# A hybrid decoder step: sample states in four row groups, small products grouped, first slice reloaded

## The chip, the cores and the metric

One core of a Trainium2 chip runs the whole step. The metric is the device time of one execution in microseconds, as the median of several runs.

## The reference

One layer on 256 prompt tokens and 8 samples of 8 tokens, 320 columns in all, of width 2048. Nine conditioning vectors go through a weight of 2048 x 12288 and give scales, shifts and gates for every feature. The layer then does the following:

```python
h = rmsnorm(x, g_pre_mix) * (1 + sc1) + sh1
q, k, v, g, u, vs = split(h @ w_in)            # six parts of 1024
o, S = retention(rotary(q), rotary(k), v, s0)  # 8 heads of 128; S = S*gamma^n + k^T v
vn = layernorm(gelu(vs), ln_g, ln_b)
m = concat([silu(g) * layernorm(o), gelu(u) * spatial_gate(vn)]) @ w_o
x = x + gt1 * rmsnorm(m, g_post_mix)
h2 = rmsnorm(x, g_pre_ffn) * (1 + sc2) + sh2
x = x + gt2 * rmsnorm(square(relu(h2 @ w_ff1)) @ w_ff2, g_post_ffn)
```

The outputs are x for prompt and samples, the retention states S of the prompt and of each of the 8 samples, and vn of the samples. A sample's new state is its old one times gamma to the 8, plus the sum over its 8 tokens of k (with a decay) times v.

## The kernel before, in words

Everything is kept with features on the 128 partitions and the 320 tokens as columns. A large product (`mm3`, line 320) is in three parts: weight and activation are each split into a high and a low half of the type fp32r, and high by high, high by low and low by high are added up in a bank of PSUM. A weight piece of up to 128 x 2048 is loaded into one of two raw buffers; `half_w` (line 294) has ScalarE cast 1024 columns of it (`wh`) and VectorE subtract that from the raw ones (`wl`), in one of three pairs of buffers. Main tiles take four banks of PSUM in turn (`new_acc`), the adaptive weights have one, and all small products share three (`small`).

The input projection runs over slices of its 16 row blocks, of 1, 2, 5 and 8 blocks (`CHUNKS`), and in each slice over 40 column tiles (`N_ORDER`); partial sums are kept in `z` and added up by VectorE. In the last slice a tile is done when its sum is, and `after_tile` (line 631) starts what depends on it: the spatial gate, and after tiles 13, 19, 25 and 31 the retention of a pair of heads (`ret_pair`, line 501). In between, `steps` loads pieces of the adaptive weights, and when four are there `flush` (line 255) issues their products, 16 calls in four column groups of the array, then VectorE's transposition of the result (`ada_drain`), four small products that sum it (`ada_sums`, tile `adaT`) and the scaling (`ada_scale`).

`ret_pair` does for each of two heads: rotation of q and k, transposes of v (`pv`) and k (`pk`), scores (`sc`), outputs (`po`), statistics. At its end come the sample states: for each two of the eight samples GpSimd masks the transposed v by sample (`ve`), TensorE multiplies it with the transposed k, 64 rows for each head (`pn`), and VectorE adds the result to the old state (line 580). After every second pair `ret_norm` (line 596) normalises and transposes the outputs, one head after the other.

`first_slice` (line 673) is the first of the four slices: five pieces of eight tiles, each in a raw buffer of its own of which it fills half, loaded and cast when the tile before has been issued.

A planner (the tile framework) orders each engine's instructions: it simulates times and takes ready work by its place in the program. `tc.high_priority` lets work go earlier (`ahead()` by 500 places), `tc.keep_in_program_order` fixes an instruction behind those fixed before it, and `tc.issue_after(i)` puts instructions behind i on its engine. Each engine's queue, and SyncE's queue of transfers, is then worked off in that order. Most calls go through helpers, so the profile shows line 112 for `tt`, 324 to 326 for `mm3` and 300 for the cast. A matmul in fp32 is two instructions in the trace, and a transpose in fp32 one.

Of the kernel before, what the change touches and what calls it, by code (L numbers as in the profile page):

```python
# [8 lines left out]
F32 = mybir.dt.float32  # L9
# [72 lines left out]
def hybrid_step(ctx: ExitStack, tc, A, O):  # L82
# [66 lines left out]
    bm = cst[:, 208:240].rearrange("p (q b) -> p q b", q=4)  # L149
# [72 lines left out]
    def ada_finish(feats, acc):  # L222
        ada_scale(*ada_sums(*ada_drain(feats, acc)))

    def ada_sums(feats, part):

        nf = len(feats)
        ncol = P * nf
        pv = part[:, :ncol].rearrange("p (i q r) -> p i q r", i=nf, q=4)
        pt = small("adaT")  # L230
        for q in range(4):
            PE.matmul(pt[32 * q : 32 * q + 32, : 9 * nf], sel, pv[:, :, q, 0:9], start=True, stop=True, tile_position=(0, 32 * q))  # L232
        return feats, pt

    def ada_scale(feats, pt):
# [12 lines left out]
    class Ada:  # L248


        def __init__(self, groups):
            self.left = list(groups)
            self.ws = []

        def flush(self, pin=False):
            if self.ws and len(self.ws) == len(self.left[0]):
                feats = self.left.pop(0)
                acc = ps_ada.tile([P, 512], F32, tag="ada", name=nm("ada"))
                with tc.high_priority():
                    ada_products(feats, self.ws, acc, pin)  # L260
                ada_finish(feats, acc)
                self.ws = []

        def products(self, acc):

            feats = self.left.pop(0)
            assert len(self.ws) == 4
            ada_products(feats, self.ws, acc)
            self.ws = []
            return feats, acc  # L270

# [229 lines left out]
    def ret_pair(qkv, pr, o, mv):  # L501

        kts, vts = slot("kts"), slot("vts")
        os_ = slot("os")
        s0s, s0qs = [], []
        for e in range(2):
            h = 2 * pr + e
            q, k, v = qkv[e]
# [10 lines left out]
            pv = small("pv")  # L519
            for t in range(2):  # L520
                PE.transpose(pv[:, P * t : P * (t + 1)], v[:, P * t : P * (t + 1)], ident)
            PE.transpose(pv[:nr, 256:384], v[:, c0:T], ident)
            vt = slot("vt")
            V.tensor_copy(vt[:, :256], pv[:, :256])
            V.tensor_copy(vts[rw, :128], pv[rw, 256:384])
# [3 lines left out]
            PE.transpose(pk[:nr, 256:384], k[:, c0:T], ident)  # L529
            kt = slot("kt")  # L530
            for t in range(2):
                S.activation(kt[:, P * t : P * (t + 1)], pk[:, P * t : P * (t + 1)], AF.Copy, scale=sdec[:, 2 * h + t : 2 * h + t + 1])
# [33 lines left out]
            s0s.append(s0)  # L566
            s0qs.append(s0q)
        for i in range(4):
            ve = slot("ve")
            tt(ve[:, :256].rearrange("p (b e) -> p b e", b=2), vts[:, :128].unsqueeze(1).broadcast_to([P, 2, P]),  # L570
               bm[:, pr, 2 * i : 2 * i + 2].unsqueeze(2).broadcast_to([P, 2, P]), ALU.mult, G)
            pns = [small("pn") for _ in range(2)]
            for e in range(2):
                rw = slice(64 * e, 64 * e + 64)
                PE.matmul(pns[e][:, :256], kts[rw, :128], ve[rw, :256], start=True, stop=True)  # L575
            for e in range(2):
                h = 2 * pr + e
                g8 = float((1.0 - 2.0 ** (-5.0 - h)) ** NS)
                sb = s0s[e][i][:, :256]
                V.scalar_tensor_tensor(out=sb, in0=sb, scalar=g8, in1=pns[e][:, :256], op0=ALU.mult, op1=ALU.add)  # L580
                if i == 3:
                    nc.sync.dma_start(O["ss"][h], s0qs[e][:, :, :256])
        return os_

    later = []
# [10 lines left out]
    def ret_norm(hs, o, oss, mv):  # L596
        rs = tp.tile([P, 12], F32, tag="rs12", name=nm("rs12"))
        rsqrt_(rs, mv[:].rearrange("p h t c -> p (h t) c")[:, :, 1], 12)
        for h in hs:
            os_ = oss[(h % 4) // 2]  # L600
            pt = small("oT")
            for t in range(3):
                src = o[h][:, P * t : P * (t + 1)] if t < 2 else os_[:, P * (h % 2) : P * (h % 2) + P]
                i = 3 * (h % 4) + t
                V.tensor_scalar(src, src, mv[:, h % 4, t, 0:1], rs[:, i : i + 1], op0=ALU.subtract, op1=ALU.mult)
                PE.transpose(pt[:, P * t : P * (t + 1)], src, ident)
            ot = slot("oT")
            S.copy(ot[:, :TP], pt[:, :TP])
            V.tensor_copy(ijs(ot[:, TP:]), rows_ijs(pt[:, 256:384]))
            oT[h] = ot  # L610


    z = {}
# [59 lines left out]
    def first_slice():  # L673

        nt = _per_piece(0)
        mod1(0, V, True)
        ws = [w_in_piece(0, last_ins[0].ins), w_in_piece(1)]
        steps(ada_a, 3)
        for ti, f in enumerate(N_ORDER):
            if ti % nt == 0 and nt <= ti < ZT - nt:  # L680
                ws.append(w_in_piece(ti // nt + 1))
            if ti == nt:
                steps(ada_a, 1)
            if ti == 21:
                ada_a.flush(True)
                steps(ada_a, 2)
            if ti in (28, 31):
                mod1(len(hx), V, True)
            if ti == 30:
                ws.append(w_in_piece(ZT // nt))  # L690
            if ti == 35:
                ada_a.flush(True)
                steps(ada_a, 2)
            acc = new_acc()
            mm3(acc, ws[ti // nt][ti % nt], hx[0], True, True)
            z[f] = slot("z")
            if ti % 3 == 2:
                V.tensor_copy(z[f], acc[:, :T])
            else:
                S.copy(z[f], acc[:, :T])  # L700
        return ws[-1]

    w0 = first_slice()
    piece = -(-ZT // _per_piece(0))
# [224 lines left out]
    for c in range(NC_FF):  # L929
        act = [None] * KB  # L930

        def done_1(m, acc):
            rl, a = slot("rl"), slot("a")
            if c == 0 and m < 8:
                u = us[m] if m < 4 else evict_1(acc)
                tt(u[:, :T], u[:, :T], r2, ALU.mult)
                tt(sam(u), sam(u), u[:, T + 1 : T + 9].unsqueeze(2).broadcast_to([P, NB, NS]), ALU.add)
                S.activation(rl[:, :TP], u[:, :TP], AF.Relu, bias=u[:, T : T + 1])
                S.activation(rl[:, TP:], u[:, TP:T], AF.Relu)
            else:  # L940
                S.activation(rl, acc[:, :T], AF.Relu)  # L941
            tt(a, rl, rl, ALU.mult, G)
            act[m] = split(a)

        if c == 0:
            steps(ada_c, 4)
            for i in range(4):
                done_1(i, acc_1[i])
            h2 = []

            def extra(n):
                steps(ada_c, 1)
                for f in range(len(h2), min(len(h2) + n, KB)):
                    h2.append(modulate(x1[f], r2, A2, SH2, f))

            project("w_ff1", 0, 8, hs, nat, (4,), lambda: extra(2), done_1, 4)
            project("w_ff1", 0, KB, h2, nat, (8,), lambda: extra(4), done_1, 8)
        else:
            project("w_ff1", 16 * c, KB, h2, nat, (), lambda: None, done_1)

        def done_2(m, acc):
            if c == 0:
                if m == 0:
                    steps(ada_c, 100)
                if m % 4 == 0:
# [11 lines left out]
    assert not ada_c.left  # L977
# [9 lines left out]
def _consts():  # L987
# [24 lines left out]
            cst[:, 128 + 2 * h + t] = gam[h] ** (TP - 1 - (P * t + np.arange(P))) * sc  # L1012
        cst[:, 144 + 8 * h : 152 + 8 * h] = gam[h] ** (np.arange(NS) + 1.0)
    for pr in range(4):
        for b in range(NB):
            for e in range(2):
                col = np.where(sb == b, gam[2 * pr + e] ** (NS - 1.0 - ss), 0.0) * sc
                cst[64 * e : 64 * e + 64, 208 + 8 * pr + b] = col

    tri = np.zeros((P, 192))  # L1020
    tri[:, :P] = np.arange(P)[None, :] >= np.arange(P)[:, None]
# [87 lines left out]
```

## Time and profile before

| | |
|---|---|
| median of 3 runs | 1573.48 us (1573.41 to 1573.91) |
| profiled execution | 1572.06 us |
| its span, first to last instruction | 1570.1 us |
| mean granted TensorE clock | 0.995 |
| TensorE busy | 1540.7 us |
| VectorE busy | 817.9 us |
| ScalarE busy | 591.3 us |
| GpSimd busy | 174.3 us |

Busy time counts an engine as busy while one of its instructions is recorded; matmuls are recorded with their fill and drain, so that neighbours overlap. The time between the starts of two neighbours shows what one costs.

### The profile page before, as it was taken

To read this page: it belongs to the slowest core of one execution; us is meant where nothing else is said; L and a number is where in the kernel's file an instruction comes from. 1 tells how busy PE (TensorE), PEld (TensorE's weight loads), DVE (VectorE), ACT (ScalarE), POOL (GpSimd) and SP (SyncE) were. 2 spreads that over 40 slices of the span, in tenths; PEclk is the share of its full clock that TensorE was granted. 3 is DMA by queue.
4 is the path that set the end of the run, shared out by engine and by line. 5 is a ranking of instruction groups with operands and counts; after the bars stand their busy time and mean duration, and the time that the engine had idled before them with its cause. 6 is when DMAs were issued, how large, how long until landed. Compare 5 with 4: busy or idle time off the path is not lost.

```text
span 1570.1 us, 25814 instructions
## 1 busy us (share of the span) xinstructions
PE 1540.7 (98%) x10852; PEld 1441.7 (92%) x10852; DVE 817.9 (52%) x1367; ACT 591.3 (38%) x891; POOL 174.3 (11%) x198
## 2 busy tenths in 40 slices
PE   8999999999999999999999999999999999999995
PEld 6798898888899998789999999999999999999995
DVE  5776566677744446676433344444444444444555
ACT  5332236233433334454433344322344223443331
POOL 0000000001000111044100121000112000121210
PEclk9999999999999999999999999999999999999998
DMA  8988886765777635884434344443434444343442
GB/s 354 379 309 325 312 333 237 251 245 184 275 287 276 265 134 202 322 314 168 147 149 160 137 161 143 153 154 142 161 138 158 148 148 158 138 161 139 157 149 80
DMA packets 57156, 323.92 MB, mean 206 GB/s; under 512 B 5584, under 2 KB 18128, under 8 KB 22096
## 3 DMA queue, kind: packets, MB, share of 16 engines
q1 hardware_dynamic: 56464, 320.98, 54.9%
q8 instruction: 85, 1.39, 0.3%
q10 hardware_dynamic: 576, 1.29, 0.2%
q14 instruction: 31, 0.25, 0.0%
HBM read 314.65 MB, written 7.60 MB: 205 GB/s over the span
## 4 chain that ended last, share of the span: by engine, by line
PE 90%; issue 4%; DVE 2%; POOL 1%; DMA 1%; ACT 1%; SPq 0%; DVEq 0%; POOLq 0%; ACTq 0%
PE acc L324 27%; PE acc L326 27%; PE acc L325 27%; PE ada L204 5%; POOL mt L112 1%; DVE f L112 1%; PE pn L575 1%; DMA adaw<-in_w_ada_dram 1%; DMA x<-in_x_dram 1%; DVE wl L112 0%; POOL a L112 0%; DVE z L112 0%; PE gate L469 0%; PE po L553 0%; PE adaT L232 0%
## 5 line engine op out<-in xcount | busy, mean ns | idle before, releaser
L324 PE MATMUL acc<-hi,wh 128*128 128x320 f32 x2944 | 913.1, 310 | 2.6 <-ACT wh L300 1.5
L326 PE MATMUL acc<-hi,wl 128*128 128x320 f32 x2944 | 910.6, 310 | 1.1 <-DVE wl L112 1.0
L325 PE MATMUL acc<-lo,wh 128*128 128x320 f32 x2944 | 910.7, 310 | 0.0
L112 DVE TENSOR_TENSOR wl<-raw,wh 128x1024 fp32r<-128x1024 f32 (+1 forms) x386 | 470.7, 1220 | 477.3 <-ACT wh L300 462.6
L300 ACT CAST wh<-raw 128x1024 fp32r<-128x1024 f32 (+1 forms) x386 | 402.9, 1045 | 731.7 <-PE acc L325 679.9
L324 PEld LDWEIGHTS acc<-hi,wh 128*128 128x128 f32 x2944 | 553.1, 188 | 13.5 <-issue 7.0
L326 PEld LDWEIGHTS acc<-hi,wl 128*128 128x128 f32 x2944 | 553.0, 188 | 8.9 <-issue 6.7
L325 PEld LDWEIGHTS acc<-lo,wh 128*128 128x128 f32 x2944 | 553.0, 188 | 4.3 <-issue 3.9
L112 POOL TENSOR_TENSOR a<-rl 128x320 f32<-128x320 f32 x64 | 84.2, 1315 | 683.3 <-ACT rl L941 631.1
L204 PE MATMUL ada<-adaw,csil 128*32 128x512 f32 (+1 forms) x800 | 88.0, 578 | 1.2 <-DMA adaw<-in_w_ada_dram 1.2
L112 DVE TENSOR_TENSOR z<-z,acc 128x320 f32<-128x320 f32 x120 | 57.3, 485 | 55.9 <-PE acc L326 55.3
L112 POOL TENSOR_TENSOR sq<-sq,sq 128x320 f32<-128x320 f32 x28 | 39.5, 1411 | 279.7 <-ACT sq L779 279.6
L112 DVE TENSOR_TENSOR lo<-a,hi 128x320 fp32r<-128x320 f32 x64 | 32.1, 502 | 67.9 <-ACT hi L333 67.9
L204 PEld LDWEIGHTS ada<-adaw,csil 128*32 128x32 f32 x800 | 23.6, 109 | 47.3 <-issue 43.6
L333 ACT CAST hi<-a 128x320 fp32r<-128x320 f32 x64 | 29.4, 459 | 90.1 <-POOL a L112 90.1
L112 DVE TENSOR_TENSOR f<-f,acc 128x320 f32<-128x320 f32 x48 | 23.4, 488 | 68.2 <-PE acc L326 68.2
L325 PE MATMUL acc<-lx,wh 128*128 128x330 f32 x128 | 40.5, 317 | 0.6 <-DVE lx L112 0.6
L326 PE MATMUL acc<-hx,wl 128*128 128x330 f32 x128 | 40.6, 318 | 0.0
L324 PE MATMUL acc<-hx,wh 128*128 128x330 f32 x128 | 39.1, 320 | 0.0
L112 POOL TENSOR_TENSOR ve<-vts,cst 128x256 f32<-128x256 f32 x16 | 14.0, 898 | 175.7 <-PE sc L537 74.7
L112 POOL TENSOR_TENSOR mt<-mt,A 128x64 f32<-128x64 f32 x23 | 11.2, 485 | 177.5 <-DVE A L246 176.0
L326 PEld LDWEIGHTS acc<-hx,wl 128*128 128x128 f32 x128 | 24.2, 189 | 2.6 <-issue 2.5
(183 smaller groups left out, 716.6 us busy)
## 6 DMA issues: line engine op xcount, KB each, us to landing
raw<-in_w_ff_dram SPq DMA_DIRECT2D x128, 1024.0 KB, 4.8
adaw<-in_w_ada_dram SPq DMA_DIRECT2D x96, 1024.0 KB, 7.8
raw<-in_w_in_dram SPq DMA_DIRECT2D x33, 1024.0 KB, 5.7
raw<-in_w_o_dram SPq DMA_DIRECT2D x16, 1024.0 KB, 4.8
raw<-in_w_in_dram SPq DMA_DIRECT2D x13, 960.0 KB, 6.0
s<-in_s_dram SPq DMA_DIRECT2D x8, 512.0 KB, 5.8
out_ss_dram<-s SPq DMA_DIRECT2D x8, 512.0 KB, 4.0
x<-in_x_dram SPq DMA_DIRECT2D x4, 640.0 KB, 6.7
```

Source lines behind the costliest of these rows:

```text
L112: return (eng or V).tensor_tensor(out=out, in0=a, in1=b, op=op)
L204: mm = PE.matmul(acc[32 * j : 32 * j + 32, :ncol], csil[:, kb, :], ws[kb // nk][:, kb % nk * ncol : (kb % nk + 1) * ncol], start=i < 4, st ...
L300: ins = S.copy(wh[:, :n], r)
L324: PE.matmul(acc[:, :n], wh, ah, start=start, stop=False)
L325: PE.matmul(acc[:, :n], wh, al, start=False, stop=False)
L326: PE.matmul(acc[:, :n], wl, ah, start=False, stop=stop)
L333: S.copy(hi, src)
L575: PE.matmul(pns[e][:, :256], kts[rw, :128], ve[rw, :256], start=True, stop=True)
```

## The change

Four things are changed.

In `ret_pair`, the sample states are multiplied in four row groups of 32 rows, each of which holds the four samples of one half of one head. ScalarE makes four masks of 128 columns for each pair (`bm` has four columns for each pair now), each of which serves all row groups. Products go to three small banks and, as the fourth, one bank of the main tiles, 512 columns each; VectorE updates the states in four instructions of 512 columns, at a higher priority. The transposes of k are put before those of v, which are kept in program order.

In `Ada`, a lazy instance (`ada_b` and `ada_c`) issues the small sums of one batch right behind the products of the next one, kept in program order.

In `ret_norm`, six transposes of two heads are issued together, the last one first.

In `first_slice`, pieces are loaded two to a raw buffer, four ahead; the adaptive loads are put between them; casts are issued at given tiles, behind the latest copies of results on their engines.

```diff
@@ Ada
+        def sums(self, pin=False):
+            if self.drained:
+                ada_scale(*ada_sums(*self.drained, pin))
+            self.drained = None
...
                 with tc.high_priority():
                     ada_products(feats, self.ws, acc, pin)
-                ada_finish(feats, acc)
+                if self.lazy:
+                    with tc.high_priority():
+                        self.sums(True)
+                    self.drained = ada_drain(feats, acc)
+                else:
+                    ada_finish(feats, acc)
...
-    ada_a, ada_b, ada_c = Ada(g_pre), Ada(g_gt1 + g_ffn), Ada(g_gt2)
+    ada_a, ada_b, ada_c = Ada(g_pre), Ada(g_gt1 + g_ffn, True), Ada(g_gt2, True)
@@ ret_pair
-        for i in range(4):
-            ve = slot("ve")
-            tt(ve[:, :256].rearrange("p (b e) -> p b e", b=2), vts[:, :128].unsqueeze(1).broadcast_to([P, 2, P]),
-               bm[:, pr, 2 * i : 2 * i + 2].unsqueeze(2).broadcast_to([P, 2, P]), ALU.mult, G)
-            pns = [small("pn") for _ in range(2)]
-            for e in range(2):
-                rw = slice(64 * e, 64 * e + 64)
-                PE.matmul(pns[e][:, :256], kts[rw, :128], ve[rw, :256], start=True, stop=True)
...
+        ve = [slot("ve")[:, :256].rearrange("p (b e) -> p b e", b=2) for _ in range(2)]
+        for j in range(4):
+            S.activation(ve[j // 2][:, j % 2, :], vts[:, :128], AF.Copy, scale=bm[:, pr, j : j + 1])
+        pns = [small("pn") for _ in range(3)] + [new_acc()]
+        for c in range(2):
+            for g in range(4):
+                rg = slice(32 * g, 32 * g + 32)
+                PE.matmul(pns[g][:, 256 * c : 256 * c + 256], kts[rg, :128], ve[c][rg].rearrange("p b e -> p (b e)"),
+                               start=True, stop=True, tile_position=(32 * g, 0))
+        for e in (1, 0):
+            h = 2 * pr + e
+            g8 = float((1.0 - 2.0 ** (-5.0 - h)) ** NS)
+            with ahead():
+                for i in (1, 0):
+                    sb = s0qs[e][:, 2 * i : 2 * i + 2, :256]
+                    V.scalar_tensor_tensor(out=sb, in0=sb, scalar=g8, in1=pns[2 * e + i].rearrange("p (b e) -> p b e", b=2), op0=ALU.mult, op1=ALU.add)
+            nc.sync.dma_start(O["ss"][h], s0qs[e][:, :, :256])
@@ first_slice
-        ws = [w_in_piece(0, last_ins[0].ins), w_in_piece(1)]
-        steps(ada_a, 3)
+        bufs = [wp.tile([P, 2048], F32, tag="raw", bufs=NRAW, name=nm("raw")) for _ in range(2)]
...
+        for i in range(2):
+            load(i)
+        steps(ada_a, 2)
+        for i in range(2, 4):
+            load(i)
+        steps(ada_a, 2)
+        ws = [half_w(bufs[0], 8 * i, behind=last_ins[0].ins) for i in range(2)]
...
+            with tc.issue_after(copies[0].ins), tc.issue_after(copies[2].ins):
+                return half_w(w, c0)
...
-            if ti == 21:
+            if ti in (14, 21):
+                ws.append(split_later(bufs[1], 8 * len(ws) - 16))
+            if ti == 16:
+                bufs.append(wp.tile([P, 2048], F32, tag="raw", bufs=NRAW, name=nm("raw")))
+                load(4)
+            if ti == 23:
                 ada_a.flush(True)
                 steps(ada_a, 2)
```

## Rows read from the trace of the kernel before

**Rows 1.** The page's head and its first part: busy us, share of span, instructions.
```profile
span 1570.1 us, 25814 instructions
...
PE 1540.7 (98%) x10852; PEld 1441.7 (92%) x10852; DVE 817.9 (52%) x1367; ACT 591.3 (38%) x891; POOL 174.3 (11%) x198
```

**Rows 2.** The page's chain of waits, shares of the span by engine.
```profile
PE 90%; issue 4%; DVE 2%; POOL 1%; DMA 1%; ACT 1%; SPq 0%; DVEq 0%; POOLq 0%; ACTq 0%
```

**Rows 3.** Windows: length, busy us of PE, PEld, DVE, ACT, POOL; clock, DMA, GB/s.
```profile
30.00:33.00 3.00, 3.00 (x23) 1.97 (x27) 1.17 (x3) 2.22 (x4) 0.00 (x0) 1.00 0.54 186
...
800.00:1200.00 400.00, 400.00 (x2734) 400.00 (x2733) 161.41 (x159) 146.58 (x184) 41.10 (x30) 1.00 0.42 150
```

**Rows 4.** Groups of instructions: busy us, mean ns, idle time before, releasers.
```profile
L112 POOL TENSOR_TENSOR ve<-vts,cst 128x256 f32<-128x256 f32 x16 | 14.0, 898 | 175.7 <-PE sc L537 74.7 <-DVE vts L525 66.5 <-issue 34.1
L575 PE MATMUL pn<-ve,kts 64*128 64x256 f32 x64 | 13.8, 418 | 0.4 <-DVE s L580 0.2
...
L580 DVE SCALAR_TENSOR_TENSOR s<-s,pn 128x256 f32<-128x256 f32 x32 | 12.4, 415 | 0.9 <-PE pn L575 0.4
...
L532 ACT ACTIVATE kt<-pk,cst 128x128 f32<-128x128 f32 x16 | 5.0, 361 | 7.0 <-PE pk L529 5.5 <-issue 1.5
```

**Rows 5.** TensorE in order of time at state products: start, length (us), engine, line, operation.
```profile
280.97 0.49 PE L575 MATMUL pn<-ve,kts 64*128 64x256 f32 x2
...
280.97 1.13 PE L575 MATMUL pn<-ve,kts 64*128 64x256 f32 x6
...
361.52 3.60 PE L575 MATMUL pn<-ve,kts 64*128 64x256 f32 x16
365.04 0.41 PE L324 MATMUL acc<-hi,wh 128*128 128x320 f32 x1
```

**Rows 6.** VectorE, then ScalarE, in order of time at the third pair's products.
```profile
362.70 1.99 DVE L580 SCALAR_TENSOR_TENSOR s<-s,pn 128x256 f32<-128x256 f32 x5
...
365.01 0.75 DVE L580 SCALAR_TENSOR_TENSOR s<-s,pn 128x256 f32<-128x256 f32 x2
...
361.01 0.37 ACT L557 COPY o<-po 128x256 f32<-128x256 f32 x1 [3.02 <-PE po L553]
```

**Rows 7.** Chain of waits in order of time: one adaptive batch (start, us).
```profile
287.22 3.57 PE ada L204 x32
```

**Rows 8.** TensorE around a lone group of sums, one beside a batch, and all.
```profile
424.17 0.31 PE L326 MATMUL acc<-hi,wl 128*128 128x320 f32 x1
424.41 0.27 PE L232 MATMUL adaT<-part,cst 128*32 128x36 f32 x8
...
424.86 0.30 PE L325 MATMUL acc<-lo,wh 128*128 128x320 f32 x1
...
696.73 0.27 PE L232 MATMUL adaT<-part,cst 128*32 128x36 f32 x8
697.00 3.64 PE L204 MATMUL ada<-adaw,csil 128*32 128x512 f32 x32
...
L232 PE MATMUL adaT<-part,cst x128: 200/212/222, 240.1 to 769.1; 128*32 128x36 f32 x128
```

**Rows 9.** TensorE at transposes: three of v together; first and last of twelve.
```profile
264.76 0.38 PE L521 MATMUL pv<-cst,z 128*128 128x128 f32 x2
...
265.01 0.39 PE L324 MATMUL acc<-hi,wh 128*128 128x320 f32 x1
...
328.93 0.30 PE L606 MATMUL oT<-cst,o 128*128 128x128 f32 x1
...
332.25 0.39 PE L326 MATMUL acc<-hi,wl 128*128 128x320 f32 x1
```

**Rows 10.** TensorE in the first slice, at its third piece.
```profile
28.69 0.41 PE L324 MATMUL acc<-hi,wh 128*128 128x320 f32 x1 [1.48 <-ACT wh L300]
...
29.95 0.55 PE L326 MATMUL acc<-hi,wl 128*128 128x320 f32 x2 [0.42 <-DVE wl L112]
```

**Rows 11.** ScalarE in the second slice, at its second piece.
```profile
56.40 1.99 ACT L300 CAST wh<-raw 128x1024 fp32r<-128x1024 f32 x2 [6.13 <-DMA raw<-in_w_in_dram]
```

More of the change, by code (lines that the diff above doesn't have):

```diff
@@ L148, in hybrid_step @@
     crs = cst[:, 144:208].rearrange("p (h s) -> p h s", h=H)
-    bm = cst[:, 208:240].rearrange("p (q b) -> p q b", q=4)
+    bm = cst[:, 208:224].rearrange("p (q j) -> p q j", q=4)
     bada = vec[:, 0:96]
@@ L223, in ada_finish, with ada_sums @@
         ada_scale(*ada_sums(*ada_drain(feats, acc)))
-    def ada_sums(feats, part):
+    def ada_sums(feats, part, pin=False):
         nf = len(feats)
@@ L231, in ada_sums @@
         for q in range(4):
-            PE.matmul(pt[32 * q : 32 * q + 32, : 9 * nf], sel, pv[:, :, q, 0:9], start=True, stop=True, tile_position=(0, 32 * q))
+            mm = PE.matmul(pt[32 * q : 32 * q + 32, : 9 * nf], sel, pv[:, :, q, 0:9], start=True, stop=True, tile_position=(0, 32 * q))
+            if pin and q == 0:
+                tc.keep_in_program_order(mm)
         return feats, pt
@@ L248, in hybrid_step, with __init__ @@
     class Ada:
-        def __init__(self, groups):
+        def __init__(self, groups, lazy=False):
             self.left = list(groups)
             self.ws = []
+            self.lazy = lazy
+            self.drained = None
+        def sums(self, pin=False):
+            if self.drained:
+                ada_scale(*ada_sums(*self.drained, pin))
+            self.drained = None
         def flush(self, pin=False):
@@ L268, in products @@
             ada_products(feats, self.ws, acc)
+            self.sums(True)
             self.ws = []
@@ L504, in ret_pair @@
         os_ = slot("os")
-        s0s, s0qs = [], []
+        s0qs = []
         for e in range(2):
@@ L518, in ret_pair @@
             nr = 64 if e == 0 else 128
[L519 to L525, printed above, removed]
             pk = small("pk")
@@ L529, in ret_pair @@
             PE.transpose(pk[:nr, 256:384], k[:, c0:T], ident)
+            pv = small("pv")
+            for t in range(2):
+                tc.keep_in_program_order(PE.transpose(pv[:, P * t : P * (t + 1)], v[:, P * t : P * (t + 1)], ident))
+            tc.keep_in_program_order(PE.transpose(pv[:nr, 256:384], v[:, c0:T], ident))
+            vt = slot("vt")
+            V.tensor_copy(vt[:, :256], pv[:, :256])
+            V.tensor_copy(vts[rw, :128], pv[rw, 256:384])
             kt = slot("kt")
@@ L565, in ret_pair @@
             V.bn_aggr(m_[:, 2, :], s6[:, 2, :])
-            s0s.append(s0)
             s0qs.append(s0q)
-        for i in range(4):
-            ve = slot("ve")
-            tt(ve[:, :256].rearrange("p (b e) -> p b e", b=2), vts[:, :128].unsqueeze(1).broadcast_to([P, 2, P]),
-               bm[:, pr, 2 * i : 2 * i + 2].unsqueeze(2).broadcast_to([P, 2, P]), ALU.mult, G)
-            pns = [small("pn") for _ in range(2)]
-            for e in range(2):
-                rw = slice(64 * e, 64 * e + 64)
-                PE.matmul(pns[e][:, :256], kts[rw, :128], ve[rw, :256], start=True, stop=True)
[L576 to L582, printed above, removed]
+        ve = [slot("ve")[:, :256].rearrange("p (b e) -> p b e", b=2) for _ in range(2)]
[15 more added lines that the diff above has]
+            nc.sync.dma_start(O["ss"][h], s0qs[e][:, :, :256])
         return os_
@@ L598, in ret_norm @@
         rsqrt_(rs, mv[:].rearrange("p h t c -> p (h t) c")[:, :, 1], 12)
[L599 to L610, printed above, removed]
+        for two in (hs[:2], hs[2:]):
+            srcs = []
+            for h in two:
+                for t in range(3):
+                    src = o[h][:, P * t : P * (t + 1)] if t < 2 else oss[(h % 4) // 2][:, P * (h % 2) : P * (h % 2) + P]
+                    i = 3 * (h % 4) + t
+                    V.tensor_scalar(src, src, mv[:, h % 4, t, 0:1], rs[:, i : i + 1], op0=ALU.subtract, op1=ALU.mult)
+                    srcs.append(src)
+            pts = [small("oT") for _ in two]
+            for i in range(5, -1, -1):
+                tc.keep_in_program_order(PE.transpose(pts[i // 3][:, P * (i % 3) : P * (i % 3 + 1)], srcs[i], ident))
+            for h, pt in zip(two, pts):
+                ot = slot("oT")
+                S.copy(ot[:, :TP], pt[:, :TP])
+                V.tensor_copy(ijs(ot[:, TP:]), rows_ijs(pt[:, 256:384]))
+                oT[h] = ot
     z = {}
@@ L697, in first_slice @@
             if ti % 3 == 2:
-                V.tensor_copy(z[f], acc[:, :T])
+                copies[2] = V.tensor_copy(z[f], acc[:, :T])
             else:
-                S.copy(z[f], acc[:, :T])
-        return ws[-1]
+                copies[0] = S.copy(z[f], acc[:, :T])
+        return ws[-2] + ws[-1]
     w0 = first_slice()
@@ L964, in done_2 @@
                     steps(ada_c, 100)
+                    ada_c.sums()
                 if m % 4 == 0:
@@ L975, in hybrid_step @@
         project("w_ff2", 16 * c, KB, act, nat, (), lambda: None, done_2)
-    assert not ada_c.left
+    assert not (ada_c.left or ada_c.drained)
     rf = mean_rsqrt(sums["f"])
@@ L1014, in _consts @@
     for pr in range(4):
-        for b in range(NB):
+        for j in range(4):
             for e in range(2):
-                col = np.where(sb == b, gam[2 * pr + e] ** (NS - 1.0 - ss), 0.0) * sc
-                cst[64 * e : 64 * e + 64, 208 + 8 * pr + b] = col
+                col = np.where(sb % 4 == j, gam[2 * pr + e] ** (NS - 1.0 - ss), 0.0) * sc
+                cst[64 * e : 64 * e + 64, 208 + 4 * pr + j] = col
     tri = np.zeros((P, 192))
```

22 lines of the change are left out of this document (14 added, 8 removed).

## The prediction

> **What bounds the kernel now.** I read the head of the page first, then the chain of waits, then windows, then the order of instructions on TensorE. The reader should see in the head that TensorE is busy for 1540.7 of 1570.1 us [rows 1], and in the chain that 90% of the time leads back to it [rows 2]: what is taken from its queue comes off the end, and what is taken from another engine doesn't, unless TensorE waits for it. Busy time alone is no measure of a matmul's price, since matmuls overlap in the record; starts are. In the quiet stretch from 800 to 1200 us, 2734 matmuls start in 400 us, 0.146 us apart [rows 3]. That is the price of one large product; every start that comes later than 0.146 us behind the one before it is either another product or a loss. So I went through the queue for those places.
>
> The profiled execution took 1572.06 us (a span of 1570.1 and 2.0 around it); the median of the runs is 1573.48, 1.4 us more. I make the sum against the first and add 1.4 at the end.
>
> **Part 1: sample states.** Each of the four head pairs sends 8 products of 64 rows, two instructions each, 64 in all [rows 4]. In the third pair they occupy the queue from 361.52 to 365.04, where the next large product starts: 3.52 us [rows 5]. The others read the same way are 3.58, 3.41 (one large product inside taken out) and 3.53, 14.04 in all; their recorded busy time is 13.8 [rows 4].
>
> Why 3.5? The price of a pass first: an adaptive batch, four products at a time in four column groups, has 32 instructions of 512 columns in 3.57 us [rows 7], 0.446 for each four, so 0.22 for 256 columns. Sixteen such passes one after another would be 3.57 us. But the first two instructions of pair 1, one for each head, both stand within a window of 0.02 us, and the first six have ended after 1.13 us where six in a row take 1.34 [rows 5]: two row halves run side by side when nothing holds them. Behind that the queue keeps step with VectorE, whose eight updates of 415 ns (3.32 us) give the small banks back two at a time [rows 4, 6]. So today's price is the drain's, not the array's.
>
> After the change there are again 8 products, 16 instructions, but in four row groups and four different banks, and none of them needs a bank to come back. Nothing shows four row groups here; two row groups and four column groups are shown. I take four at once: four passes of 0.22, 0.89, and 0.1 for the first weights, 1.0 per pair. Bounds: two at once give 8 x 0.22 + 0.1 = 1.9; one after another 3.6. Gain 14.04 - 4.0 = 10.0 us; by the bounds 6.4 and nothing.
>
> The Trainium skill (TensorE: Matmul & The Clock Gate, Part 3, Measured speedup vs the span model) gives 3.07 times, not 4, for four row tiles. By it the 16 passes (3.57 us) would take 1.16 us, and the gain would be 9.4 us. No run so far shows four row groups.
>
> The masks go from POOL (16 of 898 ns) to ScalarE, four copies of 128 columns for each pair; the nearest row is 361 ns for a scaled copy of that size, so 1.44 us [rows 4]. They need only the transposed v, and ScalarE is idle for 3.02 us in front of its copy of the outputs at 361.01 [rows 6], so I cost them at nothing; uncovered they cost up to 1.44 a pair. VectorE makes 4 updates of 512 columns in place of 8 of 256: each between 415 and 830 ns, 1.7 to 3.3 us a pair, no more than now; they are put ahead, so a few additions of main tiles come up to 3.3 us later. The borrowed bank leaves three for main tiles; a tile of eight blocks lasts 24 x 0.146 = 3.5 us, so that isn't late. What is late next is the output bank: three small banks are wanted at once, and one is free only when ScalarE has copied it (0.37 and its companion). Large products can be put there; I take 0, with up to 0.6 a pair.
>
> **Part 2: the small sums of the adaptive weights.** A lone group of eight costs more than itself: from the large product at 424.17 to the one at 424.86 there are 0.69 us, of which two large products explain 0.29, so the visit costs 0.40 [rows 8]. Beside the weight products it costs 0.27 (696.73 to 697.00) [rows 8], and as little as 0.20 if nothing is waited for. Sixteen groups stand between 240.1 and 769.1 [rows 8]. Of these two belong to the two late batches, which stay as they are, four stand beside other small products already, and the last stays alone. Nine visits, 0.13 to 0.20 each: 1.2 to 1.8 us, and I take 1.8. The sums read data that was drained a whole batch earlier, so I expect no wait.
>
> **Part 3: order within the pairs.** Twelve normalised transposes spread between large products take 328.93 to 332.25; 13 large products are 1.90 of these 3.32 us, so 0.118 each. Three together (264.76 to 265.01) cost 0.25, and 0.09 for the late product behind them: 0.113 each [rows 9]. Six together save nothing; I take 0, +-0.5 for both halves. Putting k's transposes before v's moves VectorE's two copies of v behind k's rotation; large products fill that, 0 +-1.
>
> **Part 4: first slice.** The third piece's cast comes late: 1.48 us idle, then 0.42 for its low part [rows 10]. Loading pieces three and four into a second buffer needs no buffer to come free, so they land earlier. But the cast now waits for the copy of tile 13, two tiles (6 large products, 0.88 us) before its own, and takes about 1.0 (two in 1.99, [rows 11]), so I leave a wait of about 1 us: gain 0.9. It is not carried far by itself. The next slice's second piece lands at 56.4, when ScalarE has been idle 6.13 us for it [rows 11]: there transfers are the bound. DMA is at 0.54 in 30 to 33 us [rows 3], because loads wait until TensorE has used the second adaptive batch. That batch moves from tile 21 to tile 23, which puts its loads back by 0.88 us and takes most of the gain, yet those loads also find no piece ahead of them. Bounds: 3.1 gained (both idle times and the late loads) to 1.5 lost; I take 0.8 gained.
>
> **Sum.** 10.0 + 1.8 + 0 + 0.8 = 12.6. 1572.06 - 12.6 = 1559.5, and 1.4 for the median: 1560.9 us.
>
> **Rivals.**
> (a) Only part of the state products' gain arrives: two row groups at a time, or half a drain still waited for. 1.9 in place of 1.0 a pair: 3.6 less, 1564.5; with 0.6 of waiting, 1566.9. For it: two groups are all that is shown.
> (b) Nothing of it arrives: the groups run one after another, or TensorE stands behind them until VectorE has drained the banks (1.0 + 2.5 is today's 3.5). Gain 2.6: 1570.9. The Trainium skill (TensorEngine Tiling (Array Packing), Performance Considerations, PSUM Bottleneck) says that tiling speeds up TensorE but not the evacuation of PSUM. For it: today's stretch is paced by just that. Against: after these products nothing in the queue needs those banks for a while, and large products have their own.
> (c) Slower: TensorE's queue is in order, and if the planner's times are off it stands in front of the state products for masks (1.44) and output copy (0.37) and behind them for the borrowed and small banks (up to 3.32). 1.0 + 5.1 = 6.1 in place of 3.51, +2.6 for each of four pairs, 10.4; less the other 2.6, 7.8 slower: 1581.3. It decides from 3.2 us of waiting a pair on. Against: ScalarE's idle time and the lone main bank that is lent.
> (d) The first slice frees its transfers too: 2 to 3 us more, 1558.
>
> **Chances.** Forecast 60% (its own range 1558.5 to 1563.5), (a) 15%, (b) 10%, (c) 7%, (d) 8%. The range for 8 in 10 leaves out (c), (b) and a little else: 1556.5 to 1568.5. What can be told from no change is 0.2%, 3.1 us: faster holds the forecast, (a) and (d) and little of (b), 0.84; same most of (b), 0.08; slower (c) and some unforeseen order, 0.08.
>
> **What would show it.** State products: 16 instructions in about 1 us of start to start, four starting together, and a large product right behind; wrong if they come 0.22 apart or if an idle time ended by VectorE stands there. Sums: eight small matmuls right behind each weight batch, no lone ones between 300 and 600 us. First slice: the idle of 1.48 us at about 28 us gone or near 1, and the second piece's cast at about 55.5 to 56. If the quiet stretch's pace or the tail behind 1550 us moved, something that I haven't read has changed.

## The result and the profile after

The change makes the kernel slower. The median is 1615.67 us (4 runs, 1611.72 to 1616.12) against 1573.45 us for the kernel before, a ratio of 1.0263 [1.0251, 1.0275]. The prediction was 1560.9 us, in a range that ended at 1568.5, with 0.08 for slower.

| | before | after |
|---|---|---|
| profiled execution | 1572.06 us | 1615.62 us |
| span | 1570.1 us | 1613.8 us |
| mean granted TensorE clock | 0.995 | 0.976 |
| last sums of the first two slices start | 198.81 us | 203.62 us |
| first product of line 182, after `w_o` | 610.53 us | 655.74 us |
| last sums | 769.04 us | 812.16 us |

The last three rows place the loss: 4.8 us by 199 us, 40.4 us more up to `w_o`, and nothing behind it (45.2 at line 182, 43.1 at the last sums). So the heads' stage, which was to gain 10 us, lost 40. The first 4.8 us are in part chance. Eight of the experiments below have the first slice of before, and their traces reach this landmark between 199.14 and 201.85 us; in six of them the granted clock reads 0.50 for some 3 us behind the wait near 29 us, and in the trace before it reads 1.00 there. The seven traces with the changed slice reach it between 202.27 and 204.81 us. The head of the page, to be read beside [rows 1]: TensorE is busy for 11.5 us more with as many matmuls, so some got dearer; the other 32 of the 43.7 us that the span grew are standing still.

```profile
span 1613.8 us, 25785 instructions
## 1 busy us (share of the span) xinstructions
PE 1552.2 (96%) x10852; PEld 1456.3 (90%) x10852; DVE 819.9 (51%) x1351; ACT 595.4 (37%) x907; POOL 161.4 (10%) x182
```

TensorE's own waits from 200 to 500 us, after (engine, line, who ended the wait; us in total, times, longest):

```profile
PE pk L537 <- DVE z L112: 20.1, 5, 4.5
PE po L562 <- DVE sT L112: 7.1, 8, 1.3
PE pn L590 <- ACT ve L585: 5.0, 4, 1.2
PE adaT L232 <- DVE s L598: 0.8, 1, 0.8
```

The same view of the kernel before has three lines that come to 1.1 us:

```profile
PE pk L528 <- DVE z L112: 0.6, 2, 0.4
PE pk L528 <- DVE q_pad L112: 0.3, 1, 0.3
PE pn L575 <- DVE s L580: 0.2, 1, 0.2
```

33 us of waits are four times the same picture. This is TensorE in the second pair (start, length, engine, line, operation; in brackets the idle time before it and what ended it), from the last large product in front of the pair to the first behind it:

```profile
324.00 0.31 PE L342 MATMUL acc<-hi,wl 128*128 128x320 f32 x1
324.14 0.38 PE L537 MATMUL pk<-cst,z 128*128 128x128 f32 x2
...
327.13 0.49 PE L562 MATMUL po<-vt,sT 128*128 128x128 f32 x2 [1.26 <-DVE sT L112]
...
328.41 0.65 PE L569 MATMUL po<-s,q_pad 128*32 128x128 f32 x16
333.57 0.66 PE L537 MATMUL pk<-cst,z 128*128 128x128 f32 x2 [4.52 <-DVE z L112]
334.03 0.42 PE L538 MATMUL pk<-cst,z 128*128 128x128 f32 x1
334.24 0.63 PE L541 MATMUL pv<-cst,z 128*128 128x128 f32 x2
...
337.21 0.80 PE L562 MATMUL po<-vt,sT 128*128 128x128 f32 x2 [0.52 <-DVE sT L112]
...
341.84 0.80 PE L590 MATMUL pn<-ve,kts 32*128 32x256 f32 x3 [1.25 <-ACT ve L585]
341.86 0.79 PE L590 MATMUL acc<-ve,kts 32*128 32x256 f32 x1
...
343.85 0.63 PE L340 MATMUL acc<-hi,wh 128*128 128x320 f32 x1
344.29 0.47 PE L341 MATMUL acc<-lo,wh 128*128 128x320 f32 x1
344.55 0.47 PE L342 MATMUL acc<-hi,wl 128*128 128x320 f32 x1
```

In 19.7 us there is not one large product. Before, 25 to 29 of them stand between the outputs of the first head (line 553) and the transposes of the second (line 528), and others between scores and outputs; they covered the chain that now lies open: ScalarE's copies for the rotation, VectorE's rotation, transposes, scores, masks, outputs, masks of v. From the start of the last output product of the first head to the transposes of k of the second it is 4.8 us in both kernels (313.62 to 318.42 before, 328.78 to 333.57 after): the chain is no longer than it was, it only has no cover.

The products that covered it were those of the tiles written behind the pair. One of the three lines of a large product, counted from the start to the first transposes of the second pair, before and after, and then VectorE's read of the lent bank:

```profile
L324 PE MATMUL acc<-hi,wh 128*128 128x320 f32 x480 | 149.6, 313 | 2.3 <-ACT wh L300 1.5 <-DVE z L112 0.4 <-ACT hi L347 0.3
L340 PE MATMUL acc<-hi,wh 128*128 128x320 f32 x480 | 151.1, 316 | 4.3 <-ACT z L745 1.9 <-ACT wh L316 1.5 <-DVE z L112 0.4
345.82 0.68 DVE L598 SCALAR_TENSOR_TENSOR s<-s,acc 128x512 f32<-128x512 f32 x1
```

In both kernels 480 of them have run, 320 of the first three slices and 160 of the first twenty tiles of the last one, which are those that the pair needs. Before, 51 large products of the next tiles then stand between these transposes and the first state product (48 to 61 in the four pairs); after, none in any pair. The next tile starts at 343.85, right behind the state products, and doesn't wait for the lent bank to be read (345.82 to 346.50).

The rows of the second pair show a second price: transposes are 0.21 us apart (334.03 to 334.24) where they were 0.11 [rows 9], and large products 0.27 apart where 0.146 is the price [rows 3]. Windows of the same stretch (length, TensorE busy, granted clock, DMA share, GB/s):

```profile
330.00:334.00 4.00, 0.43 (x2) 0.56 0.01 3
334.00:344.00 10.00, 8.23 (x53) 0.50 0.01 2
344.00:348.00 4.00, 4.00 (x17) 0.55 0.20 69
348.00:352.00 4.00, 4.00 (x38) 1.00 0.82 267
```

TensorE stood still for 4.5 us up to 333.57; from 334 to 344 us, through the second head, the granted clock is 0.50 of full speed, the level of 1.2 GHz, and it is back at 1.00 by 348 us. Over 100 us it reads as follows (columns as in [rows 3]; the kernel before has clock 1.00 and TensorE busy for 98.82 us in the second of these windows):

```profile
200.00:300.00 100.00, 89.62 (x620) 78.03 (x619) 57.76 (x134) 42.97 (x79) 2.80 (x5) 0.91 0.57 211
300.00:400.00 100.00, 84.92 (x592) 74.94 (x592) 60.33 (x151) 31.61 (x66) 0.00 (x0) 0.86 0.55 199
```

The size adds up. At full clock and without waits the small products of such a pair take 7.8 us (the starts in the same pair of the kernel of experiment 9); the four blocks of the kernel after take 22.0, 19.7, 18.1 and 19.7 us, 48.3 more than four times that. In front of the first block TensorE stood another 2.2 us, and behind the four blocks large products took 6.1 us more than 0.146 each. Less the gains of the sums (3.6, experiment 7) and of the states (14.04 - 4 x 1.08 = 9.7), that makes some 43 us; the landmarks show 40.4.

### The profile page after: what moved, and what is told of

Its sections match the earlier page's. It is cut to its first block, busy times and chain, and to the rows that moved or that the text cites. A ratio compares the mean times of both kernels' runs of the same rounds, so it can differ in the third digit from the quotient of the medians.

```text
span 1613.8 us, 25785 instructions
## 1 busy us (share of the span) xinstructions
PE 1552.2 (96%) x10852; PEld 1456.3 (90%) x10852; DVE 819.9 (51%) x1351; ACT 595.4 (37%) x907; POOL 161.4 (10%) x182
## 4 chain that ended last, share of the span: by engine, by line
PE 75%; DVE 2%; ACT 1%; issue 1%; DMA 1%; POOL 0%; DVEq 0%; SPq 0%; POOLq 0%
PE acc L340 23%; PE acc L341 23%; PE acc L342 23%; PE ada L204 2%; DVE f L112 1%; DMA adaw<-in_w_ada_dram 1%; PE pn L590 0%; DVE wl L112 0%; PE po L569 0%; DVE z L112 0%; PE oT L626 0%; PE po L562 0%; ACT sw L499 0%; ACT sw L498 0%; PE po L565 0%
## 5 line engine op out<-in xcount | busy, mean ns | idle before, releaser
L340 PEld LDWEIGHTS acc<-hx,wh 128*128 128x128 f32 x128 | 23.7, 189 | 3.0 <-issue 1.0
L219 DVE STREAM_TRANSPOSE part<-ada 128x512 f32<-128x512 f32 (+1 forms) x25 | 17.2, 690 | 17.7 <-PE ada L204 17.7
```

What stands on the lines that cost most here:

```text
L219: V.transpose(part[:, :ncol], acc[:, :ncol])
L340: PE.matmul(acc[:, :n], wh, ah, start=start, stop=False)
```

## The experiments

Theory: the main bank lent to the states takes its place in the rotation of the four where `ret_pair` is written down, long before its products can run, and the main tiles written after it are held back, so that nothing is left to cover the pair's chain. Experiment 1 was forecast with three tiles that may still go ahead; the count above says that none does. Rivals: the pinned transposes; the granted clock; the state products themselves; the first slice.

**1. Another bank** (`e1_ada_bank`): the changed kernel, but the fourth bank is that of the adaptive weights.

```diff
-        pns = [small("pn") for _ in range(3)] + [new_acc()]
+        pns = [small("pn") for _ in range(3)] + [ps_ada.tile([P, 512], F32, tag="ada", name=nm("ada"))]
```

> The changed kernel with one word altered: the fourth bank of the state products is the adaptive weights' bank instead of one of the main tiles' four. Theory 1 (the lent bank has its place in the rotation of the main banks, so that main tiles can run only three tiles ahead of the state products, and TensorE stands for the rest of a pair's chain): the stalls of 4.5 us before k's transposes go, and the clock stays at 2.4 GHz; the loss of 4.8 us in the first 200 us stays, and the gains of the state products (about 10) and sums (1.7) show: about 1567 us. Theory 2 (the fixed order of v's transposes keeps large products out): within 5 us of the changed kernel's 1615.7.

Measured: 1569.28 us, ratio 0.9975 [0.9965, 0.9985], clock 0.993. One line takes away 46 us; it is 2 us above the forecast. The waits of the pairs' chains shrink to 1.6 us, and a new one stands ahead:

```profile
PE ada L204 <- DVE s L598: 5.5, 3, 1.9
PE pk L537 <- DVE z L112: 0.9, 4, 0.2
PE po L562 <- DVE sT L112: 0.7, 1, 0.7
```

The state products, now with large products on both sides, show what they cost by themselves: 1.07 us from 280.91 to the next large product at 281.98, four starting together.

```profile
280.91 0.49 PE L590 MATMUL pn<-ve,kts 32*128 32x256 f32 x3
280.93 0.48 PE L590 MATMUL ada<-ve,kts 32*128 32x256 f32 x1
...
281.68 0.37 PE L590 MATMUL ada<-ve,kts 32*128 32x256 f32 x1
281.98 0.41 PE L340 MATMUL acc<-hi,wh 128*128 128x320 f32 x1
```

**2. No pins** (`e2_no_pin`): the changed kernel, v's transposes not kept in program order.

```diff
-                tc.keep_in_program_order(PE.transpose(pv[:, P * t : P * (t + 1)], v[:, P * t : P * (t + 1)], ident))
+                PE.transpose(pv[:, P * t : P * (t + 1)], v[:, P * t : P * (t + 1)], ident)
```

> The changed kernel without the fixed program order on v's transposes, the lent main bank kept. Theory 1: 1611 to 1620 us, as the changed kernel. Theory 2: the pairs open up again, about 1570 us.

Measured: 1613.53 us, ratio 1.0261 [1.0247, 1.0275]. The three waits of the pair are the same to the tenth (20.1, 7.1, 5.0), and one of 2.1 us at the normalisation is new. The pins are not the cause.

**3. The lent bank alone** (`e3_bank_before`): the kernel before, but one of its last two state banks is a main bank.

```diff
-            pns = [small("pn") for _ in range(2)]
+            pns = [small("pn"), new_acc() if i == 3 else small("pn")]
```

> The kernel before with one edit: of the eight banks that a pair's state products take, the last but none but the very last products' (fourth two samples, second head) is one of the main tiles' banks. Nothing else is changed, so the products keep their 64 rows and their price. Theory 1: this alone brings the stalls, 1605 to 1625 us. Theory 2: 1573 us, within 3.

Measured: 1617.61 us, ratio 1.0289 [1.0273, 1.0304]. Nothing else of the change is in this kernel, and it has the whole loss, with waits of the same kind, and again without a large product between a pair's first transposes and its first state products:

```profile
PE pk L528 <- DVE z L112: 14.8, 4, 4.4
PE po L546 <- DVE sT L112: 5.6, 8, 1.0
PE pk L528 <- DVE q_pad L112: 4.3, 1, 4.3
```

**4. The first slice alone** (`e4_slice_alone`): the kernel before with the changed `first_slice` as in the diff of the change.

> The kernel before with the changed first slice alone. From the trace of the changed kernel, in which the last sums before the last slice stand 4.8 us later: 1578 us. Rival (the loss is waited for anyway later in the slices that are bound by transfers, and given back): 1573 to 1575. My forecast before the result (0.8 us gained): 1572.7.

Measured: 1574.41 us, ratio 1.0007 [0.9998, 1.0016]: no gain that can be told from none. That is the rival's number; the 1578 worked out from the 4.8 us missed.

**5. The bank asked for later** (`e5_states_later`): the changed kernel with the old first slice; the states are written down three tiles after their pair.

```diff
+        def states():
...
+        states_due.append(states)
@@ after_tile
+        if ti > 13 + 2 and (ti - 8 - 3) % 6 == 5 and states_due:
+            states_due.pop(0)()
```

> The changed kernel with two edits: the state products of a pair are written into the program three tiles later (after tiles 16, 22, 28 and 34), so that the main bank that they borrow comes three places later in the rotation; and the first slice is that of before. Theory 1 (the place in the rotation is all that is wrong with the lent bank): the stalls go, the state products cost 1.08 us a pair as with the adaptive bank (9.7 gained against 14.04), and nothing waits for that bank behind them; with the sums (1.7) 11.4 less than before, 1561.6 us. Rival (a main bank that is lent costs main tiles in any place): above 1570 us.

Measured: 1575.88 us, ratio 1.0013 [1.0005, 1.0022]. Still a main bank, and some 40 us less than the change; but theory 1's 1561.6 missed by 14 us, and the number lies in the rival's range. The trace tells what is left of each: in front of each pair's state products exactly three more tiles have run, and no wait at the transposes of k or the outputs is over 0.3 us. The first and third pair are clean (1.08 and 1.07 us); in the second and fourth, where `ret_norm` is written ahead of the late states, its transposes stall (line 631, beside line 232), and the granted clock is 0.50 for 10 us near these places:

```profile
PE oT L631 <- DVE os L627: 3.4, 2, 1.7
PE adaT L232 <- DVE s L600: 3.3, 2, 2.3
```

**6. The wait filled** (`e6_filled_wait`): the changed kernel with 36 idle products, 72 instructions, pinned ahead of the second head's transposes of k.

```diff
+            if e == 1:
+                keep_warm(36)
```

> The changed kernel with 36 idle products (about 4 us, their result is not used) on TensorE in front of the second head's transposes, where it stands 4.5 us. The wait stays as long; only TensorE's work in it is added. If half the clock behind each wait is a part of the loss: the second head's block and the products behind it cost about 5 us less a pair, 1595 to 1600 us. If the wait alone is the loss: 1615.

Measured: 1617.45 us, ratio 1.0278 [1.0262, 1.0293], with a clock of 0.992. It won nothing, and by the number the wait alone would be the loss. The rows say more. It kept the clock, but for 6.8 us behind the first pair (0.50 from 287 to 293.6 us):

```profile
329.38 0.64 PE L573 MATMUL po<-s,q_pad 128*32 128x128 f32 x16
329.95 8.30 PE L132 MATMUL idle<-ones,thirty 128*128 128x128 f32 x72
338.09 0.38 PE L539 MATMUL pk<-cst,z 128*128 128x128 f32 x2
...
344.65 0.42 PE L340 MATMUL acc<-hi,wh 128*128 128x320 f32 x1
```

The filler took 8.1 us, twice what was expected, where 4.6 stood idle between the same starts, 3.5 too many; from the second head's transposes to the next large product it is 6.6 us in place of 10.3, 3.7 saved. So the half clock is worth over 3 us a pair beside the waits, but this filler was too long to show it in the time, and 4.2 us went into new waits at the normalisation's transposes (line 630). One as long as the gap was not run.

**7. The late sums alone** (`e7_sums_alone`): the kernel before with the lazy `Ada` of the change.

> The kernel before with the grouped sums of the adaptive weights alone. By my step: nine lone visits less, 1.2 to 1.8 us, 1571.4. Rival (the planner moves other work and it evens out): 1573.

Measured: 1569.70 us, ratio 0.9977 [0.9968, 0.9986]: 3.6 us gained, where 1.8 was forecast.

**8. The first slice, adaptive loads first** (`e8_slice_ada_first`): experiment 4 with four adaptive loads ahead of the third and fourth piece.

```diff
-        steps(ada_a, 2)
+        steps(ada_a, 4)
         for i in range(2, 4):
             load(i)
-        steps(ada_a, 2)
```

> The kernel before with the changed first slice, in which all four adaptive pieces of the second batch are loaded in front of the third and fourth weight piece. In the changed order TensorE's queue has that batch behind 92 large products instead of 63; with this edit it stands behind 69. If its place is what costs the 3.8 us at the end of the slices in the trace: they go, 1571 to 1573.5. If late casts cost them: 1574.4, as the slice alone.

Measured: 1576.99 us, ratio 1.0023 [1.0014, 1.0032]: 2.5 us more than experiment 4, with intervals that just touch, and neither of the two forecasts. The edit didn't separate them: the third weight piece now lands at 30.07 us (25.52 in experiment 4), TensorE stands 4.0 us for its cast, and so the adaptive batch, behind 69 large products in place of 92, still starts at 36.15 us (36.05 in experiment 4).

**9. Sums and states** (`e9_sums_states`): experiment 7 with the states in four row groups; the adaptive bank is the first of the four and is drained first.

```diff
+        pns = [ps_ada.tile([P, 512], F32, tag="ada", name=nm("ada"))] + [small("pn") for _ in range(3)]
...
+        for e in (0, 1):
...
+                for i in (0, 1):
```

> The kernel before with the late sums and the states in four row groups alone; the fourth bank is the adaptive one, taken first and drained first by VectorE; first slice, transposes and normalisation as before. Theory (the place of a main bank in the rotation made the loss, and the adaptive bank's late drain was what remained of it): sums 3.7 (measured alone) + states 14.04 - 4 x 1.08 = 9.7, less up to 0.7 of waiting at each of three adaptive batches: 1560 to 1563. Rival (the remainder comes from taking three small banks at once, in front of the products): no better than with the adaptive bank last, 1566 to 1570.

Measured: 1564.66 us, ratio 0.9938 [0.9926, 0.9951], the fastest of all. That is 8.8 us less than before, where 13.4 less some waiting was expected, and between the two forecasts: at three of four pairs the next adaptive batch comes right behind the products and wants the lent bank, and in the second it then takes 5.1 us in place of 3.57 [rows 7]. The waits first:

```profile
PE ada L204 <- DVE s L598: 4.9, 3, 2.1
```

The one in the second pair, in TensorE's order of time:

```profile
318.30 1.94 PE L204 MATMUL ada<-adaw,csil 128*32 128x512 f32 x8 [2.06 <-DVE s L598]
```

**10, 11. Order and grouping** (`e10_norm_grouped`, `e11_k_first`): experiment 9 with the grouped `ret_norm`, and the changed kernel with the banks of experiment 9 and the old first slice (so with k ahead of v and the pins as well).

> The same with the six transposes of two heads issued together in the normalisation. Theory (grouping costs and saves nothing while no bank is missing): within 1 us of the version without it. Rival (six pinned transposes wait for VectorE's normalisation of the last input, as beside the late states): 3.8 us at each of two heads pairs that are normalised, 4 to 8 us slower than the version without it.

> The changed kernel with the adaptive bank first and drained first, and the old first slice: against the version before it in this set it has k's transposes ahead of v's, with v's pinned. Theory: within 1.5 us of that version, near 1562. Rival (the order within the pair costs something of its own once the banks are right): 2 us or more slower than it.

Measured: 1566.88 us, 0.9948 [0.9934, 0.9961], and 1567.16 us, 0.9956 [0.9940, 0.9971]. The medians are 2.2 and 2.5 us above that of experiment 9, but the intervals overlap with its own: a cost of grouping or order isn't shown, and no gain either. Experiment 11 is 0.3 us above experiment 10.

**12. The first slice with free casts** (`e12_slice_free`): experiment 4 without the two conditions on the casts.

```diff
-            with tc.issue_after(copies[0].ins), tc.issue_after(copies[2].ins):
-                return half_w(w, c0)
+            return half_w(w, c0)
```

> The kernel before with the changed first slice, but its casts not held behind the copies of results. Theory (the casts held behind copies are what costs in the first slice): the third piece's wait of 1.8 us goes, 2 us less than with the casts held, 1572 to 1573. Rival (the transfers' order costs, not the casts): as with them held, 1574 to 1575.

Measured: 1574.64 us, ratio 1.0007 [0.9998, 1.0015], the same as with the casts held. The theory of the held casts falls: the third piece's cast starts at 27.69 us here, 27.60 in experiment 4 and 27.59 before, behind the same copy each time.

**13, 14. The main bank later, normalisation behind it** (`e13_main_bank_later`, `e14_main_bank_later_norm`): experiment 7 with the states in four row groups, a main bank as in the change, written down three tiles later, and `ret_norm` behind them; then with `ret_norm` grouped.

```diff
+        def both():
+            states()
+            ret_norm(hs, o, oss, mv)
```

> The kernel before with the late sums and the states in four row groups with the main bank lent as in the change, but asked for three tiles later, and the normalisation of each second pair behind the states; first slice and the rest as before. Theory (what counts is how many large products of main tiles stand between the lent bank's place in the rotation and its products; the normalisation in front of the late states made the stalls of the odd pairs): no stall, sums 3.7 and states 9.7 gained, 1560 to 1562. Rival (a lent main bank stalls TensorE wherever it is asked for): as with the states later alone, 1570 to 1576.

> The same with the six transposes of two heads issued together. Theory (they stall only where they stand in front of the states): within 1.5 us of the version without it, 1560 to 1563. Rival (six pinned transposes wait for VectorE by themselves): 3 to 8 us slower than it.

Measured: 1569.84 us, 0.9975 [0.9965, 0.9985], and 1568.79 us, 0.9975 [0.9966, 0.9984]. The loss of some 40 us is gone with a main bank still lent, but neither forecast of experiment 13 holds: the theory's 1560 to 1562 missed by 8 us, the number is at the edge of the rival's 1570 to 1576, and against experiment 7 (1569.70) nothing is left of the states' gain. As in experiment 5, exactly three more tiles have run in front of each pair's state products, and nothing of a fourth (in front of the second pair's, the line of the 480 reads 504). The transposes of the normalisation follow the states at once and want the small banks that VectorE is still draining, and once the masks are late. These waits are no longer than those of experiment 9 (4.9); but behind them the granted clock is 0.50, for 10.2 us between 200 and 600 us, where it is for 3.4 us in experiment 9. The two windows are the last rows:

```profile
PE oT L628 <- DVE s L600: 2.9, 2, 2.1
PE pn L592 <- ACT ve L587: 1.9, 1, 1.9
...
L340 PE MATMUL acc<-hi,wh 128*128 128x320 f32 x504 | 157.7, 314 | 2.3 <-ACT wh L316 1.5 <-DVE z L112 0.4 <-ACT hi L363 0.3
...
327.40:330.60 3.20, 3.20 (x15) 0.50 0.86 297
399.10:405.70 6.60, 5.77 (x37) 0.50 0.96 344
```

## Why the prediction was wrong

The step that failed is "The borrowed bank leaves three for main tiles; a tile of eight blocks lasts 24 x 0.146 = 3.5 us, so that isn't late." It counted the time in which the bank is in use, about 1 us of products and up to 3 of draining. What counts is the time from its place in the rotation to its first products, and that contains the whole pair: two heads' rotation, transposes, scores, outputs and masks, one after the other. In all that time the three banks that were left served no main tile: none of the tiles written behind the pair starts before the state products, and the next one starts right behind them (343.85 us). Experiment 3 shows the lent bank alone making the loss, experiments 1, 5 and 13 show it gone with another bank or another place in the program, and in experiments 5 and 13 the tiles that run in front of the state products are just the three that are written there. It looks as if the planner gave banks out strictly in the order in which they are asked for; how it comes to that isn't shown.

Rival (c) was the right side with the wrong place and size. It looked for waits in front of and behind the state products, up to 5.1 us a pair, with 3.2 us as the point from which they decide. Masks did end a wait there, 5.0 us in four pairs, but the larger part, 27 of 33 us, stood further ahead, at the transposes of k, nearly all of it at the second head's, and at the outputs. Its arguments against (ScalarE's idle time, a lone bank) were read from a queue that had large products in it [rows 6]: they were the cover, and the change took it away.

The other steps:

- State products: forecast 1.0 us a pair, measured 1.07 to 1.08 wherever nothing else held them (experiments 1, 5, 9). Four row groups do run side by side. Rivals (a) and the first half of (b) are out. Sixteen passes one after another stand in no trace; 3.57 us is the estimate for them. The Trainium skill (TensorE: Matmul & The Clock Gate, Part 3, Measured speedup vs the span model) has 3.07 times for four row tiles; 3.57 [rows 7] over 1.08 is 3.3 here, by this estimate a little better.
- The drain behind them, taken at nothing: this holds only where nobody wants a lent bank at once. The second half of (b) is what remains in experiments 1, 9 and 13: 0.8 to 2.1 us where an adaptive batch or a normalisation follows. The Trainium skill (TensorEngine Tiling (Array Packing), Performance Considerations, PSUM Bottleneck) says that tiling doesn't speed up the evacuation of PSUM; the waits for line 598 agree. Of the gain of 9.7 us, experiment 9 keeps about 5 (1569.70 to 1564.66).
- Sums: 1.8 forecast, 3.6 measured alone, 2.2 to 5.0 by its interval. The term was mis-sized: 3.6 in place of 1.2 to 1.8. A group beside a batch costs 0.18 from its first to the next start in the trace after, which is the price that was assumed; where the rest comes from isn't settled.
- Order within pairs: 0 forecast, and nothing else is shown; the medians of experiments 10 and 11 are 2.2 and 2.5 us above experiment 9.
- First slice: 0.8 gained was forecast, and alone it gives nothing or costs about 1 us. The third piece's first product is as late as in [rows 10]:

```profile
28.67 0.41 PE L340 MATMUL acc<-hi,wh 128*128 128x320 f32 x1 [1.46 <-ACT wh L316]
...
43.20 0.41 PE L340 MATMUL acc<-hi,wh 128*128 128x320 f32 x1 [1.93 <-ACT z L745]
```

Only VectorE's wait (0.42) went. The third piece lands earlier, as was forecast (at 25.00 us, 27.51 before), but its cast, expected about 0.9 us earlier, starts at 27.57 as before, behind a copy of results: the landing wasn't what it waited for. The last row is a new wait, at a copy of results that stands behind ScalarE's idle time for the shifts (`SH`, line 244: 5.4 us), and large products behind it are 0.27 apart up to 46 us. The sign given for the next slice failed too. Its second piece was to be cast at 55.5 to 56 us; it is cast at 59.06, in place of 56.40 [rows 11], and the adaptive loads ahead of it are issued from 37.15 us on, in place of 32.88:

```profile
37.15 12.03 SPq L294 DMA_DIRECT2D adaw<-in_w_ada_dram  x6
59.06 1.99 ACT L316 CAST wh<-raw 128x1024 fp32r<-128x1024 f32 x2 [5.53 <-DMA raw<-in_w_in_dram]
```

The step that failed here is the 0.88 us by which the second adaptive batch was to move. Written two tiles later, it stands behind 92 large products in place of 63 and starts at 36.02 us in place of 31.75, and the loads that wait for it come 4.3 us later. What that costs in the end isn't shown, since experiment 8 left the batch as late. The conditions on the casts cost nothing that shows (experiment 12). In the whole kernel the slice costs about 1 us, which can't be told from none; what makes it stays open.

## What to carry to other kernels

A buffer borrowed from a rotation cost, here, the time from the place where it is asked for to its first use, not the time for which it is used: find what has to run between the two, and count in the trace how much of the covering work written behind the request still runs before that use. Here it was none, though three buffers were left. Ask for it right before it can be used, or take it from a pool that no covering work needs, and then look at who wants it next. A queue in which small chains look free is no evidence that they stay so: name the work that covers them, and see whether the change touches that work's supplies.

## What the hardware showed

Standing still costs twice: behind 4.5 us without work, TensorE's granted clock was 0.50 for the next 10 us and more, and transposes took 0.21 us where they took 0.11. Filling the gaps kept it, but for 6.8 us (0.992 over the run), and saved 3.7 us a pair up to the next large product, but the filler was 3.5 us longer than the gap. And four row groups of 32 rows start within 0.02 us of each other, 16 instructions of 256 columns in 1.08 us, 67 ns each.
